# Building the expert-weight table from squared key differences, and conditioning in quarters inside the attention

## The chip, the cores and the metric

The kernel runs on one core of one Trainium2 chip. The metric is device microseconds of one execution, smaller being better. In the profile PE is the matrix engine, DVE the vector engine, ACT the scalar engine, POOL the gather engine and SP the engine that issues the plain DMA transfers. All five run their own instruction streams in program order and wait for one another by semaphores. PSUM is the accumulator memory that PE writes, eight banks of 128x512 float32.

## The reference

Two layers over 512 latent tokens and 256 context tokens of width 1024, float32. Each layer is a conditioned norm, attention (8 heads, 2 key heads), an output projection, a second conditioned norm and a channel mixer that picks experts by product keys:

```python
mod = jax.nn.silu(c) @ ada_w[i] + ada_b[i]          # 6 x 1024 shifts, scales, gates
h = modulate(rms_norm(x, norm1_gain[i]), sh1, sc1)
...
cand_s = (v1[..., :, None] + v2[..., None, :]).reshape(n, PEER_HEADS, PEER_TOPK * PEER_TOPK)
top_s, pos = lax.top_k(cand_s, PEER_TOPK)           # 16 of 128 x 128 experts for each of 8 heads
expert = jnp.take_along_axis(cand_i, pos, axis=-1)
g = jax.nn.softmax(top_s, axis=-1)
act = jax.nn.gelu(jnp.einsum('nhkd,nd->nhk', u_tab[expert], hb))
return jnp.einsum('nhk,nhkd->nd', g * act, v_tab[expert])
```

So every token has 128 (head, rank) slots, each with two keys of 0 to 127 (an expert is 128 times the first plus the second) and a weight g.

## The kernel before

**Layers.** A layer runs qkv, attention, the output projection, the second norm and the expert queries (`peer_q`, with the first top-k), and then mixes experts in two ways at once. The *sparse* way gathers expert rows with POOL (256 context tokens in layer 0, 128 of the 512 latent tokens in layer 1). The *dense* way multiplies all latent tokens that are left (512 in layer 0, 384 in layer 1) with all 16,384 experts: per group of 128 experts, `weights` makes the scores (`sp`, 24 matmuls into PSUM tag "S"), gelu on ACT (`act`), a product with the expert weights `Gt` on DVE, and `outputs` multiplies with the value table (`kp`, `op`). `sp` may run ahead of the rest by LEAD = 5 groups, and by as many `act` buffers as AHEAD gives (2 in layer 0, 12 in layer 1), and `Gt` must have been loaded before the first product.

**The table.** `Gt` is read back from `Gd` in DRAM, which holds for every token a 128x128 table: the sum over the 128 slots of g at (first key, second key). It is built in tiles of 128 tokens, four in layer 0 and three in layer 1, between `peer_q` and the dense work. Per tile `topk_scan` and `topk_resolve` find the slots' keys. `topk_resolve` does so in two passes, i = 0 for the first key and i = 1 for the second: ACT copies the key differences into a large tile `rep` (one buffer), DVE makes a mask `hot` and multiplies the two (2048 elements per partition each), and 16 matmuls add up the result into `keys`. `build_g` then works in rounds of TB = 8 tokens. DVE compares an iota with the keys of 8 tokens (`hot`, bf16, both key sets at once), DVE multiplies the first half with g (`first`, float32), ACT widens the second half (`second`, float32). PE multiplies the two for each token (`gm`, four tokens to a bank of PSUM tag "bg"), and three banks of four are evacuated to `gsb` by ACT, the fourth by DVE. After 32 tokens SP sends `gsb` to `Gd`.

**Conditioning.** `ada_cols` makes 2048 of the 6144 columns of `mod`: 16 loads of 512 KB, 64 matmuls `pr`, a copy `rows`, four transposes `pc` and an add. Layer 0 has groups 0 (at the start), 1 (between qkv and attention) and 2 (in the output projection); the three groups of layer 1 stand behind the first three tiles of layer 0's table.

**Order.** A scheduler in the framework orders each engine's stream when the program is built, from the program's order, its dependences and the buffers. The order is fixed from then on: an engine whose next instruction waits does nothing else.

## Time and profile before

| | us |
|---|---|
| three runs | 4041.8, 4048.7, 4053.2 (median 4048.7) |
| the profiled execution | 4048.4 |
| its span, first to last instruction | 4046.6 |
| PE busy in the span | 3753.2 (93%) |
| DVE busy | 3091.0 (76%) |
| ACT busy | 1536.2 (38%) |
| POOL busy | 1000.8 (25%) |

The span runs through these stages: conditioning and the first norm (0 to 41 us), qkv of layer 0 (41 to 172), conditioning group 1 (to 194), attention (to 336), output projection and norm (to 430), expert queries (to 605), the table (first table matmul at 629.9, last at 880.4), the dense work of layer 0 (to 2290), and in layer 1 the same up to the table (2807.7 to 2993.6) and the dense work (3016.2 to the end). A busy share over the whole span says little, since the stages have different limits, so the rows below are taken by stage. A matmul row may carry several instructions (x16): its duration is then that of the whole burst. Matmuls overlap in the pipeline, so the time that one more costs is the spacing of starts, or a window's PE time over its count, and not the mean duration of one.

### The profile page before, as it was taken

What the parts mean: (1) busy time and instruction counts of PE and PEld (TensorE: products, weight loads), DVE (VectorE), ACT (ScalarE), POOL (GpSimd) and SP (SyncE); (2) the same over time, 40 slices, a digit from 0 to 9 for tenths busy, and PEclk for the clock granted to TensorE, in tenths of its full rate; (3) what the DMA queues carried; (4) which work ended last, traced back from release to release, by engine and by line L of the source; (5) the groups of instructions that cost most, each with busy time, mean ns of one, the idle gap of its engine ahead of it and who ended that gap; (6) DMA issues with size and microseconds to landing.
All of it is one profiled execution on the core that took longest, in us unless ns stands there. A gap on an engine that the chain in (4) does not pass through costs nothing.

```text
span 4046.6 us, 52056 instructions
## 1 busy us (share of the span) xinstructions
PE 3753.2 (93%) x19384; PEld 3200.5 (79%) x19384; DVE 3091.0 (76%) x5913; ACT 1536.2 (38%) x2217; POOL 1000.8 (25%) x778
## 2 busy tenths in 40 slices
...
GB/s 176 125 1 115 58 67 268 188 188 174 297 322 316 310 320 329 324 312 317 316 317 319 250 87 52 45 77 46 154 209 245 303 301 297 296 297 297 305 261 157
DMA packets 343407, 894.08 MB, mean 221 GB/s; under 512 B 25968, under 2 KB 145904, under 8 KB 338800
## 3 DMA queue, kind: packets, MB, share of 16 engines
...
## 4 chain that ended last, share of the span: by engine, by line
PE 49%; issue 19%; DVE 13%; DMA 10%; POOL 8%; ACT 2%; POOLq 0%; SPq 0%; DVEq 0%; ACTq 0%
PE sp L170 5%; DMA gv<-v_n,idx 5%; PE sp L168 5%; PE sp L169 5%; DVE first L554 4%; POOL gv L598 4%; POOL gu L598 4%; PE pj L168 4%; PE pj L169 4%; PE pj L170 4%; DMA gu<-u_n,idx 3%; PE kp L682 2%; PE kp L683 2%; PE kp L681 2%; PE op L683 2%
## 5 line engine op out<-in xcount | busy, mean ns | idle before, releaser
L598 POOL DMA_INDIRECT gu<-u_n,idx x384 | 548.8, 1429 | 2670.0 <-DVE idx L578 964.3
L168 PE MATMUL sp<-hil,Uh 128*128 128x512 f32 (+1 forms) x2048 | 750.8, 367 | 29.8 <-ACT act L659 29.5
L169 PE MATMUL sp<-lol,Uh 128*128 128x512 f32 (+1 forms) x2048 | 751.2, 367 | 0.0
L170 PE MATMUL sp<-hil,Ul 128*128 128x512 f32 (+1 forms) x2048 | 747.0, 365 | 2.6 <-DVE Ul L162 2.6
L626 DVE SCALAR_TENSOR_TENSOR acc<-gv,w,acc 128x1024 f32<-128x1024 f32 x381 | 489.5, 1285 | 138.3 <-DMA gv<-v_n,idx 137.6
L667 ACT CAST wh<-act 128x512 fp32r<-128x512 f32 (+1 forms) x256 | 145.0, 567 | 1039.9 <-DVE act L665 1033.3
L598 POOL DMA_INDIRECT gv<-v_n,idx x384 | 448.9, 1169 | 330.8 <-DVE acc L626 220.2
L616 DVE CUSTOM_DVE_ANT_0 gu<-gu,hn 128x1024 f32<-128x1024 f32 x384 | 468.0, 1219 | 66.7 <-DMA gu<-u_n,idx 66.6
L168 PEld LDWEIGHTS sp<-hil,Uh 128*128 128x128 f32 x2048 | 387.4, 189 | 75.9 <-ACT act L659 30.2
L162 DVE TENSOR_TENSOR Ul<-Ur,Uh 128x1024 fp32r<-128x1024 f32 x256 | 312.4, 1221 | 170.8 <-ACT Uh L160 170.7
L682 PE MATMUL kp<-wh,Vl 128*128 128x512 f32 (+1 forms) x1024 | 381.9, 373 | 47.5 <-DVE Vl L162 47.2
L170 PEld LDWEIGHTS sp<-hil,Ul 128*128 128x128 f32 x2048 | 387.3, 189 | 47.1 <-DVE Ul L162 3.9
L169 PEld LDWEIGHTS sp<-lol,Uh 128*128 128x128 f32 x2048 | 387.6, 189 | 38.5
L160 ACT CAST Uh<-Ur 128x1024 fp32r<-128x1024 f32 x256 | 269.0, 1051 | 391.2 <-PE sp L169 384.5
L681 PE MATMUL kp<-wh,Vh 128*128 128x512 f32 (+1 forms) x1024 | 378.5, 370 | 0.8 <-ACT wh L667 0.7
L683 PE MATMUL kp<-wl,Vh 128*128 128x512 f32 (+1 forms) x1024 | 379.1, 370 | 0.0
L681 PE MATMUL op<-wh,Vh 128*128 128x512 f32 (+1 forms) x1024 | 371.3, 363 | 0.6 <-DVE xl L652 0.6
L683 PE MATMUL op<-wl,Vh 128*128 128x512 f32 (+1 forms) x1024 | 370.8, 362 | 0.0
L682 PE MATMUL op<-wh,Vl 128*128 128x512 f32 (+1 forms) x1024 | 370.7, 362 | 0.0
L160 ACT CAST Vh<-Vr 128x1024 fp32r<-128x1024 f32 x256 | 268.7, 1050 | 221.0 <-PE op L683 201.8
L562 PE MATMUL gm<-first,second 128*128 128x128 f32 x1792 | 239.9, 292 | 98.0 <-DVE first L554 88.1
L562 PEld LDWEIGHTS gm<-first,second 128*128 128x128 f32 x1792 | 223.9, 204 | 126.8 <-ACT second L557 79.3
...
## 6 DMA issues: line engine op xcount, KB each, us to landing
Ur<-u_t SPq DMA_DIRECT2D x256, 512.0 KB, 6.0
Vr<-v_b SPq DMA_DIRECT2D x256, 512.0 KB, 6.8
...
```

The costliest lines, as they stand in the source:

```text
L160: A.copy(hi, raw)
L162: V.tensor_tensor(lo, raw, hi, ALU.subtract)
L168: T.matmul(o, sh, mh, start=i == 0, stop=False)
L169: T.matmul(o, sh, ml, start=False, stop=False)
L170: T.matmul(o, sl, mh, start=False, stop=i == n - 1)
L562: T.matmul(po[:, i * P:(i + 1) * P], second[:, k], first[:, k], start=True, stop=True)
L598: G.indirect_dma_start(out=r, out_offset=None, in_=tab, in_offset=bass.IndirectOffsetOnAxis(ap=idx[:, s:s + 1], axis=0))
L616: V.tensor_tensor_reduce(out=r, in0=r, in1=hn, scale=1.0, scalar=0.0, op0=ALU.mult, op1=ALU.add, accum_out=sd[:, k:k + 1])
L626: V.scalar_tensor_tensor(acc[ti], r, w[:, k:k + 1], acc[ti], ALU.mult, ALU.add)
L681: T.matmul(o[:, :n], vh[:, k, ds], wh, start=start, stop=False, skip_group_check=True)
L682: T.matmul(o[:, :n], vl[:, k, ds], wh, start=False, stop=False, skip_group_check=True)
L683: T.matmul(o[:, :n], vh[:, k, ds], wl, start=False, stop=stop, skip_group_check=True)
```

## The change

Three things change.

**The table.** The one-hot rows no longer come from a comparison with an iota. The `keys` matmuls swap their operands, so that keys come out with tokens instead of slots on the partitions. Five bf16 rows per token are made from the keys k: k, the high and low part of k squared, and two rows of ones (`kd`). They go to DRAM (`kdd`) and come back for each block of 32 tokens with five rows of each of four tokens on 20 partitions (`lk`, one load for each of the two key sets). A constant matrix `sqr` holds 2a, -1, -1 and the parts of -a squared, so that one bf16 matmul `df` of 512 columns gives -(k-a) squared for four tokens. DVE reads the first bank and makes `first` = (df == 0) times g in one instruction; ACT reads the second and makes `second` = relu(df + 1). Rounds have four tokens instead of eight, `first` and `second` three buffers instead of two. The `df` banks have the PSUM tags "O" and "S", and "S" is also that of `sp`.

**Conditioning.** Group 1 of layer 0 and the three groups of layer 1 are cut into quarters (16 matmuls, four loads of 512 KB), and one quarter is placed behind every second query tile of the latent attention in layer 0, sixteen in all.

**Smaller edits.** AHEAD is 3 instead of 2 in layer 0. The pool of the weights is closed before the table is built, and `sparse_prep` loses a copy and two transposes.

```diff
-AHEAD = (2, 12)
+AHEAD = (3, 12)
...
+    def ada_quarters(todo, pool):
+        parts = [(l, grp, q) for l, grp in todo for q in range(4)]
+        loads = []
+        def load():
+            l, grp, q = parts[len(loads)]
+            raws = []
+            for j in range(4):
+                tag, n = ("wr", WR) if len(loads) % 2 == 0 else (("wh", 2), ("wl", 2))[j // 2]
+                raw = pool.tile([P, 2, CBA], F32, tag=tag, name=nm(tag), bufs=n)
+                dma(raw, ada_w[l, grp * 4 + j, :, 2 * q:2 * q + 2])
+                raws.append(raw)
+            loads.append(raws)
+        state = [0, None]
+        def step():
+            i = state[0]
+            state[0] += 1
+            if i >= len(parts):
+                return
+            if i == 0:
+                load()
+                load()
+            l, grp, q = parts[i]
+            pr = bank("S", nm("pr"), 2)
+            for kt in range(2):
+                for j in range(4):
+                    js = slice(32 * j, 32 * j + 32)
+                    T.matmul(pr[js], cst[:, 2 * q + kt], loads[i][j][:, kt], start=kt == 0, stop=kt == 1,
+                             skip_group_check=True)
+            if len(loads) < len(parts):
+                load()
+            if q == 0:
+                state[1] = pool.tile([P, CBA], F32, tag="rows", name=nm("rows"), bufs=1)
+                A.copy(state[1], pr)
+                return
+            rows = state[1]
+            V.tensor_tensor(rows, rows, pr, ALU.add)
+            if q == 3:
+                ada_spread(l, mods[l], grp, rows)
+        return step
...
 def attention(...): ... for qt in range(nt):
+                if beside and qt % 2 == 1:
+                    beside()
...
 def topk_resolve(...): ...
-                T.matmul(ps_[:, i * P:(i + 1) * P], flat(rep[:, a]), identb, start=a == 0, stop=a == 15,
+                T.matmul(ps_[:, i * P:(i + 1) * P], identb, flat(rep[:, a]), start=a == 0, stop=a == 15,
...
-    def build_g(pt, Gd, t, gp, kp):
-        ib = gp.tile([P, 2, P], BF16, tag="ib", name=nm("ib"), bufs=2)
-        A.copy(ib.rearrange("p a b -> p (a b)"), pt[:, :2 * P])
+    def build_g(pt, Gd, t, gp):
+        kd = gp.tile([P, KINDS, 2, P], BF16, tag="kd", name=nm("kd"), bufs=1)
+        both = pt[:, :2 * P].rearrange("p (m s) -> p m s", m=2)
+        A.copy(kd[:, 0], both)
+        kf = gp.tile([P, 2, P], F32, tag="kf", name=nm("kf"), bufs=1)
+        A.copy(kf, both)
+        V.tensor_tensor(kf, kf, kf, ALU.mult)
+        A.copy(kd[:, 1], kf)
+        V.tensor_tensor(kd[:, 2], kf, kd[:, 1], ALU.subtract)
+        V.memset(kd[:, 3:], 1.0)
+        kdd = dram.tile([P, KINDS, 2, P], BF16, tag="kdd", name=nm("kdd"), bufs=2)
+        dma(kdd, kd)
-        HT = TB // 2
+        NB = GB // TQ
...
         for b in range(P // GB):
             gs = gp.tile([P, NK, GB], F32, tag="gsb", name=nm("gsb"), bufs=GSB)
-            for n8 in range(GB // TB):
-                tok = slice(b * GB + n8 * TB, b * GB + (n8 + 1) * TB)
-                hot = kp.tile([P, 2, NK, TB], BF16, tag=("hot", "rep")[n8 % 2], name=nm("hot"), bufs=1)
-                V.tensor_tensor(hot, iota_t[:, None].to_broadcast([P, 2, NK, TB]),
-                                ib[:, :, None, tok].to_broadcast([P, 2, NK, TB]), ALU.is_equal)
-                first = gp.tile([P, TB, NK], F32, tag="first", name=nm("first"), bufs=2)
-                V.tensor_tensor(first, hot[:, 0].rearrange("p a t -> p t a"),
-                                gt[:, tok, None].to_broadcast([P, TB, NK]), ALU.mult)
-                second = gp.tile([P, TB, NK], F32, tag="second", name=nm("second"), bufs=2)
-                A.copy(second, hot[:, 1].rearrange("p a t -> p t a"))
-                for half in range(2):
-                    po = bank("bg", nm("gm"), 4)
-                    for i in range(HT):
-                        k = half * HT + i
-                        T.matmul(po[:, i * P:(i + 1) * P], second[:, k], first[:, k], start=True, stop=True)
-                    pending.append((po, gs, (n8 * 2 + half) * HT, b))
-                    if len(pending) > LAG:
-                        evacuate()
+            lk = gp.tile([KR + 32, NB, P], BF16, tag="lk", name=nm("lk"), bufs=2)
+            for m in range(2):
+                dma(lk[32 * m:32 * m + KR],
+                    kdd[b * GB:(b + 1) * GB, :, m].rearrange("(n t) k s -> (t k) n s", t=TQ))
+            for n4 in range(NB):
+                tok = slice(b * GB + n4 * TQ, b * GB + (n4 + 1) * TQ)
+                dif = []
+                for m, tag in enumerate(("O", "S")):
+                    d_ = bank(tag, nm("df"), 2)
+                    rows = slice(32 * m, 32 * m + KR)
+                    T.matmul(d_, lk[rows, n4], sqr[rows], start=True, stop=True)
+                    dif.append(d_)
+                first = gp.tile([P, TQ, NK], F32, tag="first", name=nm("first"), bufs=3)
+                V.scalar_tensor_tensor(first, dif[0].rearrange("p (t a) -> p t a", t=TQ), 0.0,
+                                       gt[:, tok, None].to_broadcast([P, TQ, NK]), ALU.is_equal, ALU.mult)
+                second = gp.tile([P, TQ, NK], F32, tag="second", name=nm("second"), bufs=3)
+                A.activation(second, dif[1].rearrange("p (t a) -> p t a", t=TQ), AF.Relu, bias=onec)
+                po = bank("bg", nm("gm"), 4)
+                for i in range(TQ):
+                    T.matmul(po[:, i * P:(i + 1) * P], second[:, i], first[:, i], start=True, stop=True)
+                pending.append((po, gs, n4 * TQ, b))
+                if len(pending) > LAG:
+                    evacuate()
...
-            if L == 0:
-                ada_cols(0, modT, 1, wp, ada_load(0, 1, wp, 0))
+                beside = ada_quarters([(0, 1), (1, 0), (1, 1), (1, 2)], wp)
-                attention(LAT, L, blocks_global, *r, ap, False)
+                attention(LAT, L, blocks_global, *r, ap, False, beside)
...
+        wp_es.close()
-        if last:
-            wp_es.close()
-                build_g(pt, Gd, t - c0 // P, gp, kt)
-                if not last:
-                    if t < 3:
-                        ada_cols(1, mods[1], t, wp, ada_load(1, t, wp, 0))
-        if not last:
-            kt_es.close()
-            wp_es.close()
+                build_g(pt, Gd, t - c0 // P, gp)
...
+    a = np.arange(NK)
+    aa = (a * a).astype(np.float32)
+    hi = ((aa.view(np.uint32) + 0x8000) & 0xFFFF0000).astype(np.uint32).view(np.float32)
+    kinds = np.stack([2 * a, -np.ones(NK), -np.ones(NK), -hi, hi - aa]).astype(np.float32)
+    sqk = np.zeros((TQ, KINDS, TQ, NK), np.float32)
+    for i in range(TQ):
+        sqk[i, :, i] = kinds
+    arrays["sqk"] = sqk.reshape(KR, TQ * NK)
```

**Inside a tile of the table, PE.** `gm` are the table's matmuls (x4 is four tokens) and `sp` the score matmuls of the dense work of layer 1. Before, in layer 1's second tile:

```order
L562 MATMUL gm_22085<-first_22076,second_22078 128x128 x4
L562 MATMUL gm_22097<-first_22093,second_22095 128x128 x4
L562 MATMUL gm_22103<-first_22093,second_22095 128x128 x4
L170 MATMUL sp_23132<-hil_17935,Ul_23130 128x384
L168 MATMUL sp_23132<-hil_17935,Uh_23128 128x384
L169 MATMUL sp_23132<-lol_17936,Uh_23128 128x384
L170 MATMUL sp_23132<-hil_17935,Ul_23130 128x384
L168 MATMUL sp_23132<-hil_17935,Uh_23128 128x384
L169 MATMUL sp_23132<-lol_17936,Uh_23128 128x384
L562 MATMUL gm_22115<-first_22111,second_22113 128x128 x4
L562 MATMUL gm_22121<-first_22111,second_22113 128x128 x4
```

and now, in a tile of layer 0 (LDWEIGHTS brings `lk` for the `df` matmul behind it):

```order
L623 LDWEIGHTS lk_6432
L623 MATMUL df_6492<-sqr,lk_6432 128x512
L632 MATMUL gm_6472<-first_6468,second_6470 128x128 x4
L632 MATMUL gm_6486<-first_6482,second_6484 128x128 x4
L623 LDWEIGHTS lk_6432
L623 MATMUL df_6494<-sqr,lk_6432 128x512
L623 LDWEIGHTS lk_6432
L623 MATMUL df_6506<-sqr,lk_6432 128x512
L623 LDWEIGHTS lk_6432
L623 MATMUL df_6508<-sqr,lk_6432 128x512
L623 LDWEIGHTS lk_6432
L623 MATMUL df_6520<-sqr,lk_6432 128x512
```

No `sp` stands among the `gm` or ahead of them any more, in either layer: in both, all 120 matmuls of the first five groups stand behind the last `gm`. Four `df` for the next eight tokens stand ahead of each pair of `gm`, except the `df` in tag "S" of the pair that comes next, which is first behind the pair before it.

**Inside a tile, ACT.** `gsb` is an evacuation of four tokens. Before, in layer 1:

```order
L557 CAST second_21752<-hot_21748 128x1024
L557 CAST second_21771<-hot_21767 128x1024
L541 COPY gsb_21747<-gm_21754 128x128x4
L541 COPY gsb_21747<-gm_21761 128x128x4
L541 COPY gsb_21747<-gm_21773 128x128x4
L557 CAST second_21789<-hot_21785 128x1024
L557 CAST second_21807<-hot_21803 128x1024
L541 COPY gsb_21747<-gm_21791 128x128x4
L541 COPY gsb_21747<-gm_21797 128x128x4
L541 COPY gsb_21747<-gm_21809 128x128x4
```

and now, in layer 0:

```order
L629 ACTIVATE second_6470<-df_6466,onec 128x512
L629 ACTIVATE second_6484<-df_6480,onec 128x512
L606 COPY gsb_6431<-gm_6472 128x128x4
L629 ACTIVATE second_6498<-df_6494,onec 128x512
L629 ACTIVATE second_6512<-df_6508,onec 128x512
L606 COPY gsb_6431<-gm_6500 128x128x4
L606 COPY gsb_6431<-gm_6514 128x128x4
L629 ACTIVATE second_6526<-df_6522,onec 128x512
L629 ACTIVATE second_6540<-df_6536,onec 128x512
L606 COPY gsb_6431<-gm_6528 128x128x4
```

The evacuation of a `gm` stands ahead of the `second` for the next pair, one evacuation in one pair and two in the next.

**Between two tiles, ACT and DVE.** `hot` in these rows is the large tile of `topk_resolve`. Before, in layer 1, from the evacuation to the next tile's `second`, ACT has:

```order
L489 ACT_TABLE_LOAD
L489 ACTIVATE ts_20075<-ts_20075 128x128
L160 CAST Uh_22904<-Ur_22902 128x1024
L659 ACT_TABLE_LOAD
L659 ACTIVATE act_22787<-sp_22762 128x384
L509 CAST rb_21625<-low_21619 128x128
L513 COPY hot_21649<-k_4185_21615 128x2048
L499 CAST k_4288_22013<-i_3896_20078 128x128
L530 CAST ib_21671<-keys_21627 128x256
L532 COPY gt_21673<-keys_21627 128x128
L557 CAST second_21680<-hot_21676 128x1024
L557 CAST second_21697<-hot_21693 128x1024
```

and now, in layer 0, from the last evacuation of a tile:

```order
L606 COPY gsb_6431<-gm_6528 128x128x4
L568 COPY hot_6626<-k_1394_6592 128x2048
L554 CAST k_1583_7170<-i_737_3587 128x128
L568 COPY hot_7183<-dif_7167 128x2048
L587 CAST kd_6648<-keys_6604 128x256
L589 COPY kf_6650<-keys_6604 128x256
L597 COPY gt_6658<-keys_6604 128x128
L591 CAST kd_6648<-kf_6650 128x256
L629 ACTIVATE second_6670<-df_6666,onec 128x512
```

DVE has there before, ahead of the first `first` of the next tile:

```order
L516 TENSOR_TENSOR hot_21649<-hot_21649,hot_21651 128x2048
L453 MAX_INDEX pos_20080<-ts_20079,scr_21989 128x8
L450 MAX_INDEX pos_20080<-ts_20079,cand_21971 128x8
L451 MATCH_REPLACE scr_21995<-ts_20079,cand_21971 128x72
L487 COPY gs_22001<-ts_20079 128x8
L162 TENSOR_TENSOR Ul_22833<-Ur_22829,Uh_22831 128x1024
L452 MAX ts_20079<-scr_21995 128x8
L551 TENSOR_TENSOR hot_21676<-iota_t,ib_21671 128x2048
L551 TENSOR_TENSOR hot_21693<-iota_t,ib_21671 128x2048
L554 TENSOR_TENSOR first_21678<-hot_21676,gt_21673 128x1024
```

and now:

```order
L606 COPY gsb_6431<-gm_6542 128x128x4
L571 TENSOR_TENSOR hot_6626<-hot_6626,hot_6628 128x2048
L570 TENSOR_TENSOR hot_7185<-posb_7172,first_pos 128x2048
L571 TENSOR_TENSOR hot_7183<-hot_7183,hot_7185 128x2048
L590 TENSOR_TENSOR kf_6650<-kf_6650 128x256
L570 TENSOR_TENSOR hot_7206<-rb_7180,rank 128x2048
L592 TENSOR_TENSOR kd_6648<-kf_6650,kd_6648 128x256
L593 MEMSET kd_7226 128x512
L626 SCALAR_TENSOR_TENSOR first_6668<-df_6664,gt_6658 128x512
```

The tile behind the next one (hot_7183, hot_7185, hot_7206) has its masks made here, ahead of the `kf` and `kd` instructions of the next tile (number 6648 and 6650), on both engines. On SP `kdd` is followed by two loads `lk` for each 32 tokens.

## Rows read from the trace of the kernel before

**Rows 1.** Busy time by stage (instructions in brackets), granted clock, DMA share, GB/s

```profile
core 0: us, PE busy (x) PEld busy (x) DVE busy (x) ACT busy (x) POOL busy (x), PEclk, DMA share, GB/s
193.70:336.00 142.30, 131.50 (x580) 83.64 (x579) 102.01 (x338) 85.39 (x227) 0.00 (x0) 0.99 0.04 13
629.90:880.40 250.50, 195.30 (x1355) 160.59 (x1355) 245.68 (x290) 201.87 (x196) 0.00 (x0) 0.92 0.65 196
880.40:908.00 27.60, 7.86 (x25) 6.25 (x26) 17.23 (x96) 10.37 (x15) 0.00 (x0) 0.63 0.89 304
908.00:2290.00 1382.00, 1330.59 (x5766) 1079.82 (x5765) 1121.84 (x1475) 375.10 (x504) 628.33 (x504) 0.99 0.86 304
2807.70:2993.60 185.90, 132.81 (x982) 123.73 (x983) 183.46 (x202) 153.68 (x151) 0.00 (x0) 0.96 0.50 142
2993.60:3016.20 22.60, 14.63 (x77) 13.87 (x75) 15.09 (x62) 11.96 (x17) 0.00 (x0) 0.81 0.95 312
3016.20:4046.60 1030.40, 1018.23 (x5844) 1014.46 (x5843) 789.37 (x1065) 363.19 (x490) 358.71 (x256) 1.00 0.79 276
```

**Rows 2.** Groups of instructions by shape, 605 to 3016 us: busy, mean ns | idle before

```profile
L562 PE MATMUL gm<-first,second 128*128 128x128 f32 x1792 | 239.9, 292 | 98.0 <-DVE first L554 88.1 <-DVE gsb L541 4.8 <-ACT second L557 3.4
L554 DVE TENSOR_TENSOR first<-hot,gt 128x1024 f32<-128x1024 bf16 x112 | 225.4, 2018 | 0.0
L541 ACT COPY gsb<-gm 128x512 f32<-128x512 f32 x168 | 97.3, 593 | 43.7 <-PE gm L562 41.7
L652 DVE SCALAR_TENSOR_TENSOR xl<-op,mod,xl 128x512 f32<-128x512 f32 x128 | 95.2, 744 | 17.5 <-PE op L683 17.5
L516 DVE TENSOR_TENSOR hot<-hot,hot 128x2048 bf16<-128x2048 bf16 x18 | 22.0, 1220 | 4.7 <-ACT hot L513 4.7
L513 ACT COPY hot<-k 128x2048 bf16<-128x2048 bf16 x10 | 19.0, 1898 | 4.8 <-PE keys L518 4.8
```

**Rows 3.** PE over time: start, duration, instruction [idle before <-releaser], layer 1's tiles

```profile
2856.91 2.02 PE L562 MATMUL gm<-first,second 128*128 128x128 f32 x16 [0.50 <-DVE ts L452]
...
2862.75 1.07 PE L518 MATMUL keys<-identb,hot 128*128 128x128 bf16 x16
...
2869.39 1.89 PE L518 MATMUL keys<-identb,hot 128*128 128x128 bf16 x16 [3.15 <-DVE hot L516]
...
2876.44 3.90 PE L562 MATMUL gm<-first,second 128*128 128x128 f32 x32
...
2925.05 2.02 PE L562 MATMUL gm<-first,second 128*128 128x128 f32 x16 [0.50 <-DVE first L554]
```

**Rows 4.** PE over time, start of layer 0's table

```profile
629.88 6.41 PE L562 MATMUL gm<-first,second 128*128 128x128 f32 x32 [3.51 <-DVE first L554]
```

**Rows 5.** ACT over time, between two tiles of layer 1

```profile
2871.52 0.37 ACT L530 CAST ib<-keys 128x256 bf16<-128x256 f32 x1 [3.65 <-PE keys L520]
```

**Rows 6.** ACT reading a PSUM bank with a pointer operand, by line, 41 to 336 us

```profile
L312 ACT ACTIVATE qTl<-pj,qkg 128x512 f32<-128x512 f32 x8 | 5.5, 683 | 0.0
```

**Rows 7.** Chain of waits: stores to DRAM of 512 KB and of 2048 KB

```profile
2676.07 2.84 DMA h_d<-hnat
...
881.17 10.14 DMA Gd<-gsb
```

**Rows 8.** PE over time: conditioning groups 1 and 2 of layer 0

```profile
182.20 1.80 PE L200 MATMUL pr<-wr,cst 128*32 128x512 f32 x6
...
193.17 0.66 PE L206 MATMUL pc<-ident,rows 128*128 128x128 f32 x4 [0.68 <-ACT rows L203]
...
385.33 7.07 PE L200 MATMUL pr<-ar,cst 128*32 128x512 f32 x64
```

**Rows 9.** The `sp` instructions alone by stage: PE, PEld, ACT busy, clock

```profile
629.90:880.40 250.50, 26.72 (x96) 18.34 (x96) 1.19 (x2) 0.92 0.65 196
2700.00:2807.70 107.70, 23.46 (x122) 21.41 (x122) 1.95 (x4) 0.98 0.15 47
2807.70:2993.60 185.90, 30.42 (x148) 26.64 (x149) 3.54 (x7) 0.96 0.50 142
```

44 lines of the change are left out of this document (22 added, 22 removed).

## The prediction

> **What bounds the kernel now.** I read the stage table first. In the dense work PE is nearly always busy: 1330.59 of 1382 us in layer 0 and 1018.23 of 1030.4 in layer 1 [rows 1]. One matmul less there is one matmul sooner, at 1330.59/5766 = 0.231 us for 512 columns and 1018.23/5844 = 0.174 us for 384. The latent attention too is mostly PE, 131.50 of 142.3, with 10.8 us idle. The table is another matter. In its two windows (250.5 and 185.9 us) DVE is busy for 245.68 and 183.46, PE for 195.30 and 132.81, ACT for 201.87 and 153.68 [rows 1]. In the groups, `gm` waits 98.0 us in all, 88.1 of it for `first` on DVE, and DVE has 2018 ns of `first` for eight tokens and the `hot` besides [rows 2]. So DVE sets the table's pace, and this is what the change attacks.
>
> PE's time in those windows is not all the table's. 96 `sp` (26.72 us) lie inside layer 0's table, and 122 + 148 ahead of and inside layer 1's [rows 9]: dense work done free of charge while DVE is late. They stop being free if they are pushed out.
>
> A tile's body, from the first `gm` at 2876.44 to the end of the last burst at 2925.05 + 2.02, takes 50.6 us [rows 3]. That leaves between tiles (250.5 - 4 x 50.6)/3 = 16.0 us in layer 0 and (185.9 - 3 x 50.6)/2 = 17.0 in layer 1. The gap shown, 2858.93 to 2876.44, is 17.5 [rows 3].
>
> **Part 1, a pair of `gm` (eight tokens).** A further 16 passes of `gm` cost (3.90 - 2.02) = 1.88 us [rows 3]. The four new `df` of 512 columns are priced from the `sp` spacing at 0.231 each (from the 16 `keys` of 128 columns, 1.07/16 x 4 = 0.27), so PE alone needs 1.88 + 0.92 = 2.80 a pair. DVE needs two reads of a bank, at 744 ns for an op of that form, and a share of the evacuations: it drops to half. ACT needs two `second`, at 683 ns (a read of a bank with a pointer operand) [rows 6], and one or two evacuations at 593 [rows 2]: under 2.6. By throughput PE would be the bound. But the streams have a fixed order. An evacuation stands on ACT ahead of the next pair's `second`, and `gm` of that pair needs that `second`. Where ACT evacuates the second bank of a pair, a pair takes the whole loop: `gm` 1.88, evacuation 0.59, `second` 0.68 and two handovers of some 0.1, 3.35 in all. Where DVE takes that bank, the `df` in tag "S" stands behind the `gm`: 1.88 + 0.23 + 0.68 + 0.3 = 3.1. The mean is 3.22, and a tile's body 15 x 3.22 + 1.88 = 50.2, against 50.6: **no gain**, though DVE is freed.
>
> The Trainium skill ("ScalarE: Activation LUTs", Rules for kernel authors) says to do a relu on VectorE, which it has as up to three times as fast per element in bf16. For a float32 bank of PSUM the rows say otherwise: 744 ns on DVE, 683 on ACT [rows 2, 6]. Still, by that rule `second` would leave ACT's queue, a pair would take the four DVE reads, 2.98, and the seven tiles some 25 us less, 4103 in all.
>
> **Part 2, between tiles.** The chain after the last `gm` is now: `keys` 1.07, ACT's copy 1.90, DVE's product 1.22, `keys` 1.89 [rows 2, 3], with handovers 6.6. Then ACT's copy and DVE's product for the tile behind the next, 1.90 + 1.22, which stand in front; then three small steps of at most 0.37 each [rows 5] and one more mask, 1.22, that stands between them: with handovers 6.0. Then two trips through DRAM, `kdd` and `lk`, each taken as the 512 KB store, 2.84 [rows 7]: 5.7. Then `df` and `second`, 1.2. That is 19.5, and 15.2 for the last gap of a layer, where no tile is behind the next (4.3 less). The trips are the uncertain piece, since no load in 256-byte pieces is in the trace. With `lk` at nothing the gap is 16.7; with `kdd` as slow as the 2048 KB store `Gd`, 10.14 [rows 7], it is 27. I stay with 2.84, since `kdd` has 328 KB.
>
> The Trainium skill ("DMA: Bandwidth & Descriptors", Specifications and Anatomy of one DMA) gives a fixed 2.0 us per DMA and wants 512 bytes for line rate, and the `lk` pieces have 256. Its fit would make an estimate of 2.75 + 2.09 = 4.8 us for both trips and the sum 6 us less; the row with 2.84 is in line with it, and no row shows the penalty for small pieces.
>
> Two more things belong here. In the gap PE did `sp` before, and the burst after it ran at full pace (32 in 3.90, 2876.44). Now PE has only `keys` there, and the nearest row for a start out of idleness is 629.88: 32 in 6.41 [rows 3, 4], 2.5 us more. And the first `gm` of a layer waits for kd, both trips and `df` (12.9) instead of `ib`, `hot` and `second` (5.2 from the end of the second `keys` to the `gm` at 2876.44): 7.7 later in layer 0, and in layer 1, where DVE is behind with top-k, between 2 and 7.7, taken as 5.
>
> Layer 0: 7.7 + (2 x 19.5 + 15.2 - 48.1) + 3 x 2.5 - 4 x 0.4 = **+20** (from -25 to +50). Layer 1: 5 + (34.7 - 34.1) + 2 x 2.5 - 3 x 0.4 = **+9** (from -25 to +30).
>
> **Part 3, the dense work behind the table.** The order has no `sp` ahead of the last `gm` any more, since `df` holds tag "S", and 120 behind it. In layer 0 this costs nothing. The handover there takes 27.6 us, of which PE is busy for 7.86 [rows 1], the rest being the trip of `Gd` to `Gt`, and the third `act` buffer lets 120 `sp` (27.7) run in it. **0** (to +5). In layer 1 AHEAD was 12 all along. Before, 270 + 77 = 347 `sp` are done when `kp` begins (77 in the handover, clock 0.81) [rows 1, 9]; now 120. The missing 227 come back inside a stage that is PE from end to end: 227 x 0.174 = 39.5. The handover is 22.6 long, and 120 x 0.174 = 20.9 fit. **+40** (25 to 47).
>
> **Part 4, conditioning.** A group is 64 matmuls, 7.07, and four transposes, 0.66 [rows 8]. Three groups lay inside layer 0's table, where PE had time. Now four lie in the attention, 30.9 us of PE. Group 1 no longer stands alone: 182.20 to 193.7 [rows 1, 8], and about 2 us of its matmuls before that, 13.5. Of the 10.8 us that PE idles in the attention I let them fill 6. **+11** (+5 with all 10.8 filled, +17 with none). Their transfers take 64 loads of 512 KB, 33.6 MB, which at 304 GB/s [rows 1] is 110 us, less than the stage, in which the queues now carry 13 GB/s.
>
> The copy and two transposes taken out of `sparse_prep` lie beside the dense work: 0 to -1.
>
> **The sum** starts from the profiled execution, 4048.4 us (span 4046.6 and 1.8 around it; the median of the runs is 4048.7): 4048.4 + 11 + 20 + 0 + 9 + 40 = **4128**.
>
> **Rivals.**
> *The build falls to PE's own work.* This is the reading by busy shares: DVE is the bound, PE next. The windows of the table then hold 195.30 - 26.72 (`sp`) - 23.2 (three conditioning groups) + 256 x 0.231 (`df`) = 204.5 of 250.5, and 132.81 - 30.42 (`sp` again) + 192 x 0.231 = 146.7 of 185.9 [rows 1, 8, 9]: 85 us gained. With +11 and +40 this gives 4048.4 - 85 + 51 = 4014, **faster**. It decides from about 7 us saved per tile with its gap (50 of the 85 over seven tiles). For it: 88.1 of 98.0 us of waits name `first`. Against it: the order on ACT, and a chain between tiles that PE cannot shorten. Chance 0.15.
>
> *Only the pair reaches PE's floor*, because handovers and `second` overlap better than I add them: 15 x 2.80 + 1.88 = 43.9 a tile, 6.3 less in seven tiles, 44 us: 4084. Chance 0.14.
>
> *The quarters come late.* They are sixteen waits on PE's queue with the rest of attention behind them. If each stalls by as much as one quarter's transfer (2.1 MB at 304 GB/s, 6.9 us) exceeds the two-quarter lead, some 2 us, it adds 34: 4162. For it: SP issues in order, and each load waits for a buffer that an earlier step frees. Against it: two quarters are loaded ahead and a head takes about 16 us. Chance 0.11.
>
> **How the numbers follow.** Forecast 0.60. Differences under 0.3% (12 us) cannot be told from no change. The forecast's own range, 4095 to 4160, is all slower. The first rival is faster but for a small part, the second slower or same. Faster 0.14, same 0.09, slower 0.77. The range leaves out most of the first rival and a little above the third: 4040 to 4175.
>
> **What would show it.** In the new trace: `gm` in pairs about 3.2 us apart, idle before them put down to ACT's `second` and not to DVE; DVE near half busy in the table; gaps of 17 to 24 us between tiles with only `keys` on PE; no `sp` in the table's windows; 120 `sp` in layer 1's handover and a dense stage there of about 1070 us; attention near 160 us with 16 steps of `pr`. I am wrong if pairs come 2.8 apart, if gaps are near 10, or if layer 1's dense stage does not grow.

## The result and the profile after

The changed kernel takes 4197.6 us (median of four runs, 4188.6 to 4208.7), the kernel before 4047.5 beside it: a ratio of 1.0372, 95% interval 1.0342 to 1.0402. It is slower by 150 us. The forecast was 4128, slower, with a range that ended at 4175, so the sign was right and the size about half of what came. The profiled execution took 4194.0 us, with a span of 4192.1.

The timelines of the two profiles, read at the same events, show where the time went (us from the start of each span):

| event | before | after | later by | of this, in the stage |
|---|---|---|---|---|
| conditioning in the output projection, layer 0 | 385.3 | 424.1 | 38.8 | 38.8 |
| last matmul of the expert queries, layer 0 | 603.1 | 644.8 | 41.7 | 2.9 |
| first `gm`, layer 0 | 629.9 | 679.9 | 50.0 | 8.3 |
| last `gm` ends | 880.4 | 939.5 | 59.1 | 9.1 |
| first `kp` | 908.0 | 967.4 | 59.4 | 0.3 |
| last `kp` of layer 0 | 2368.5 | 2438.2 | 69.7 | 10.3 |
| last matmul of the expert queries, layer 1 | 2772.4 | 2846.1 | 73.7 | 4.0 |
| first `gm`, layer 1 | 2807.7 | 2891.1 | 83.4 | 9.7 |
| last `gm` ends | 2993.5 | 3080.6 | 87.1 | 3.7 |
| first `kp` | 3016.2 | 3101.8 | 85.6 | -1.5 |
| last `kp` | 4040.4 | 4186.1 | 145.7 | 60.1 |

The largest shares are the dense work of layer 1 (60.1, forecast 40) and the front up to the end of the expert queries (41.7, forecast 11); the dense work of layer 0 (10.3) had no term in the forecast. The two tables, from the expert queries to the last `gm`, carry 17.4 and 13.4 and are near what was forecast. (The dense work of layer 0 ends with its last `kp`, in before at 2368.9 and not at 2290.)

The stage table of after has the same columns as [rows 1]; its first row is the latent attention.

```profile
core 0: us, PE busy (x) PEld busy (x) DVE busy (x) ACT busy (x) POOL busy (x), PEclk, DMA share, GB/s
200.90:375.00 174.10, 151.34 (x782) 80.44 (x781) 97.95 (x295) 74.38 (x188) 0.00 (x0) 1.00 0.52 189
679.90:939.50 259.60, 183.88 (x1376) 139.84 (x1376) 124.16 (x236) 147.71 (x248) 0.00 (x0) 0.91 0.44 132
939.50:967.40 27.90, 27.90 (x122) 22.43 (x121) 21.23 (x92) 16.47 (x22) 0.00 (x0) 1.00 0.83 289
2891.10:3080.60 189.50, 137.69 (x1023) 105.39 (x1023) 82.86 (x128) 108.18 (x179) 0.00 (x0) 0.91 0.43 130
3080.60:3101.80 21.20, 21.20 (x121) 20.91 (x119) 13.85 (x56) 13.89 (x19) 0.00 (x0) 1.00 0.88 312
```

DVE, busy for 245.68 of 250.5 us in layer 0's table before [rows 1], is now busy for 124.16 of 259.6: the change did what it says, DVE is free, and the table takes longer. Both handovers (rows three and five) are about as long as before (27.6 and 22.6) with PE busy throughout, on 120 `sp`. The latent attention, from 211.4 to 336 before, fills 174 us. The same view of before for that stretch and, behind it, what PE waited for in it after (us in all, times, the longest):

```profile
211.40:336.00 124.60, 115.90 (x504) 72.16 (x503) 85.35 (x273) 70.97 (x184) 0.00 (x0) 0.99 0.02 5
```

```profile
PE sc L421 <- ACT pr L438: 11.4, 7, 1.7
PE pt L453 <- DVE mx L429: 5.1, 4, 1.3
PE pr L251 <- DVE pT L460: 2.1, 4, 0.5
...
```

PE has 35.4 us more work there and idles for 22.8 instead of 8.7: the waits of the scores (`sc`) for the softmax and of the transposes (`pt`) for the maximum have grown, and new ones for the copies out of tag "S" have come. (`pr` of L438 is the softmax's tile, `pr` of L251 the accumulator of the quarters.)

Inside a tile the timeline of PE shows pairs of `gm` 3.3 us apart (start, duration, instruction, idle before), here in the first tile:

```profile
689.90 2.05 PE L632 MATMUL gm<-first,second 128*128 128x128 f32 x16 [0.73 <-ACT second L629]
691.88 0.60 PE L623 MATMUL df<-sqr,lk 20*128 20x512 bf16 x4
693.22 2.05 PE L632 MATMUL gm<-first,second 128*128 128x128 f32 x16 [0.73 <-ACT second L629]
```

In the first tile every pair takes 3.32 us; in the six others pairs of 3.32 and 3.21 us alternate, but for the slow ones at a tile's start. ACT in such a tile shows why:

```profile
776.78 0.59 ACT L606 COPY gsb<-gm 128x512 f32<-128x512 f32 x1 [0.67 <-PE gm L632]
778.05 1.27 ACT L629 ACTIVATE second<-df,onec 128x512 f32<-128x512 f32 x2 [0.69 <-PE df L623]
779.98 0.59 ACT L606 COPY gsb<-gm 128x512 f32<-128x512 f32 x1 [0.67 <-PE gm L632]
780.88 0.59 ACT L606 COPY gsb<-gm 128x512 f32<-128x512 f32 x1 [0.31 <-PE gm L632]
781.36 1.27 ACT L629 ACTIVATE second<-df,onec 128x512 f32<-128x512 f32 x2
```

Where DVE takes the pair's second bank, ACT idles for 0.69 us until PE has made the `df`, and the pair takes 3.21; where ACT takes it, `second` stands behind that evacuation, and the pair takes 3.32.

Between two tiles there is a gap of 16.8 us, first on PE, then on DVE:

```profile
734.01 1.06 PE L573 MATMUL keys<-hot,identb 128*128 128x128 bf16 x16
738.31 1.86 PE L573 MATMUL keys<-hot,identb 128*128 128x128 bf16 x16 [3.25 <-DVE hot L571]
...
749.04 1.96 PE L623 MATMUL df<-sqr,lk 20*128 20x512 bf16 x5 [8.65 <-DMA lk<-kdd]
750.97 3.78 PE L632 MATMUL gm<-first,second 128*128 128x128 f32 x16
```

```profile
744.75 0.42 DVE L592 TENSOR_TENSOR kd<-kf,kd 128x256 bf16<-128x256 f32 x1
...
747.56 0.48 DVE L593 MEMSET kd<- 128x512 bf16 x1 [2.12 <-DMA kdd<-kd]
```

The last part of `kd` is done at 745.17, `kdd` has been stored by 747.56 and `lk` is there at 749.04: 2.4 and 1.5 us for the two trips, where the forecast took 2.84 each. The burst behind the gap then takes 3.78 us for 16, against 2.05 later. The granted clock is why: in the gap PE is nearly idle (busy for 0.39 us from 740 to 749), the clock in the burst is 0.50 (1.2 GHz), and behind it 1.00 (2.4 GHz):

```profile
751.00:754.60 3.60, 3.60 (x17) 3.45 (x16) 0.69 (x1) 1.08 (x2) 0.00 (x0) 0.50 0.01 2
754.70:765.00 10.30, 8.22 (x65) 6.01 (x64) 4.84 (x8) 6.53 (x11) 0.00 (x0) 1.00 0.04 8
```

### The profile page after: what moved, and what is told of

Same layout as the page of the kernel before. It is cut to its first block, busy times and chain, and to the rows that moved or that the text cites. A ratio compares the mean times of both kernels' runs of the same rounds, so it can differ in the third digit from the quotient of the medians.

```text
span 4192.1 us, 53315 instructions
## 1 busy us (share of the span) xinstructions
PE 3837.3 (92%) x19826; PEld 3213.3 (77%) x19826; DVE 2916.6 (70%) x5949; ACT 1451.9 (35%) x2331; POOL 997.6 (24%) x777
## 3 DMA queue, kind: packets, MB, share of 16 engines
q0 software_dynamic: 110592, 402.70, 27.6%
## 5 line engine op out<-in xcount | busy, mean ns | idle before, releaser
L746 PE MATMUL op<-wh,Vh 128*128 128x512 f32 (+1 forms) x1024 | 376.4, 368 | 10.6 <-DVE xl L717 10.6
L169 DVE TENSOR_TENSOR Vl<-Vr,Vh 128x1024 fp32r<-128x1024 f32 x256 | 311.3, 1216 | 8.5 <-ACT Vh L167 8.2
```

The costliest lines, as they stand in the source:

```text
L169: V.tensor_tensor(lo, raw, hi, ALU.subtract)
L746: T.matmul(o[:, :n], vh[:, k, ds], wh, start=start, stop=False, skip_group_check=True)
```

## The experiments

Twelve kernels were run, each beside the kernel before on the same chip. Ratios are to that kernel, with their 95% intervals:

| run | median us | ratio (interval) |
|---|---|---|
| the changed kernel | 4197.6 | 1.0372 (1.0342 to 1.0402) |
| quarters_only | 4077.2 | 1.0073 (1.0056 to 1.0090) |
| table_only | 4219.4 | 1.0423 (1.0405 to 1.0440) |
| after_shift | 4194.0 | 1.0366 (1.0348 to 1.0383) |
| after_df_bg | 4166.3 | 1.0296 (1.0279 to 1.0314) |
| after_second_dve | 4204.9 | 1.0397 (1.0377 to 1.0417) |
| after_made_ahead | 4143.4 | 1.0241 (1.0218 to 1.0263) |
| after_pr_o | 4183.9 | 1.0344 (1.0322 to 1.0367) |
| combo | 4069.2 | 1.0050 (1.0024 to 1.0076) |
| after_df_ahead | 4153.4 | 1.0264 (1.0248 to 1.0280) |
| after_sparse_early | 4163.2 | 1.0289 (1.0271 to 1.0307) |
| combo_df_s0 | 4003.3 | 0.9900 (0.9885 to 0.9915) |
| before_sparse_early | 4034.0 | 0.9963 (0.9950 to 0.9975) |

**The two parts by themselves: quarters_only and table_only.** The edit of the first:

```diff
-            if L == 0:
-                ada_cols(0, modT, 1, wp, ada_load(0, 1, wp, 0))
...
+                beside = ada_quarters([(0, 1), (1, 0), (1, 1), (1, 2)], wp)
-                attention(LAT, L, blocks_global, *r, ap, False)
+                attention(LAT, L, blocks_global, *r, ap, False, beside)
...
-                        ada_cols(1, mods[1], t, wp, ada_load(1, t, wp, 0))
```

> The kernel before with the conditioning alone moved into the attention (sixteen quarters; the table as before). Theory from the trace of after: a head of the latent attention takes 21.2 us instead of 14.1 there, and the output projection's conditioning starts 38.8 us later. If the quarters alone do this, this kernel shows the same 21 us a head, about 39 us more up to the output projection, and 30 to 40 us in all, since the groups taken out of layer 0's table lay where PE had time: about 4083. Rival, the forecast's term: +11 us, about 4058. Second rival: the loss comes from something else in the changed kernel's front, and this one stays at 4047.

It measured 4077.2, some 30 us more. Its heads come 20.2 and 22.5 us apart in turn, as in after, where before they came 14.1 apart, and its first `gm` is 35.4 us later than before. Its table for layer 0 then takes 251.8 us, against 250.5: taking three conditioning groups out of it gave nothing back, which fits the rows of before, in which they lay in time that PE waited for DVE.

The second has the new `build_g`, `topk_resolve` and `sparse_prep`, and all else as before, AHEAD of 2 and the pools among it:

> The kernel before with the new table alone (conditioning where it was, AHEAD 2 and 12, pools as before; the constant sqr is staged through the tile of the sub-keys to fit the memory). Theory: what is left of after's 4195 without the 39 us of the quarters, 4156, with pairs of gm 3.3 us apart, no sp ahead of layer 1's last gm, and layer 1's dense stage some 1080 us long. Rival: the two parts hinder one another, and without the quarters it is nearer to the forecast's 4117 (4128 less 11).

It measured 4219.4, which neither side had expected: without the quarters the new table is slower still, by 22 us. The gaps of layer 0 are 36.8 to 41.4 us long (in layer 1, where no conditioning stands between tiles, 13.3 and 16.1). PE in one of them, cut:

```profile
708.19 5.50 PE L207 MATMUL pr<-wr,cst 128*32 128x512 f32 x15 [7.75 <-DMA wr<-ada_w]
...
720.24 1.06 PE L525 MATMUL keys<-hot,identb 128*128 128x128 bf16 x16
724.54 1.05 PE L525 MATMUL keys<-hot,identb 128*128 128x128 bf16 x16 [3.25 <-DVE hot L523]
```

The whole conditioning group stands on PE between the last `gm` and the next tile's `keys`, with the wait for the second half of its loads. So the quarters cost about 30 us by themselves and, with AHEAD 3 and the pools, save about 22 next to the new table; the two effects do not add.

**Where the operand lies: after_shift.**

```diff
-    onec = const.tile([P, 1], F32, name="onec")
-    V.memset(onec, 1.0)
...
-                A.activation(second, dif[1].rearrange("p (t a) -> p t a", t=TQ), AF.Relu, bias=onec)
+                A.activation(second, dif[1].rearrange("p (t a) -> p t a", t=TQ), AF.Relu, bias=ones[:, :1])
```

> The changed kernel with one constant of one column left out (relu's bias is a column of the tile of ones), so that every tile behind it lies 32 bytes lower in the memory, and the operand hi and lo of the scores again at an address that is 32 more than a multiple of 64, as before. Nothing else differs. In after's trace the sp starts are 2 to 3 per cent further apart than in before's (0.2300 against 0.2239 us in layer 0, 0.1744 against 0.1709 in layer 1, by the same count), while kp and op are not. Theory: this comes from where the operand lies; then sp goes back to before's spacing and the time falls by 3072 times 0.006 and 0.0035, some 25 us, to 4170. Rival: the spacing has another cause and stays, 4195.

The spacing went back. In 300 us of layer 1's dense work (the stage view, from 3500 to 3800), before, after and after_shift in this order:

```profile
3500.00:3800.00 300.00, 300.00 (x1727) 300.00 (x1726) 240.46 (x313) 108.19 (x148) 124.57 (x86) 1.00 0.85 298
...
3500.00:3800.00 300.00, 300.00 (x1716) 300.00 (x1715) 239.04 (x308) 107.16 (x145) 125.18 (x86) 1.00 0.85 298
...
3500.00:3800.00 300.00, 300.00 (x1727) 300.00 (x1726) 240.18 (x312) 108.27 (x146) 124.86 (x86) 1.00 0.85 300
```

The time did not go down as expected. In layer 1 the dense stage took 1072.6 us instead of 1084.3. In layer 0 PE was busy for 13.6 us less, but waited that much longer, above all for `Vl` (36.6 against 26.0). The median, 4194.0, cannot be told from 4197.6. So about 11 us of the loss lie in layer 1's `sp` by the trace, and the times do not decide it.

**The head start: after_df_bg.**

```diff
-                for m, tag in enumerate(("O", "S")):
-                    d_ = bank(tag, nm("df"), 2)
+                for m, tag in enumerate(("bg", "bg")):
+                    d_ = bank(tag, nm("df"), 4)
...
-                po = bank("bg", nm("gm"), 4)
+                po = bank("O", nm("gm"), 2)
```

> The changed kernel with the accumulator banks swapped: the squared differences take the four banks of gm, gm the two of tag O, and tag S is left to sp. In the order sp stands in the table again, one to four between the pairs, and in the gaps. Theory: layer 1's loss (58 us from first kp to the end against before) is the lost head start, so it falls away but for the part that before did ahead of the table; 45 to 60 us less, 4140 to 4150, with pairs of gm still 3.3 us apart, since sp lies in PE's waits. Rival: the pairs become longer by what sp takes (2 on average, 0.35 us), half of the gain is lost, 4165.

It measured 4166.3, 31 us under after. With tag "S" left to them, 351 `sp` stand ahead of layer 1's first `kp` (344 before, 120 in after), and from there to the last `kp` it takes 1048.1 us instead of 1084.3. Pairs stay at 3.32 us (median), so `sp` does lie in PE's waits. But the first `gm` of layer 1 comes later against the expert queries (52.3 us, 45.0 in after) and the table is 3 us longer. The lost head start is worth 36 us, near the forecast's 40. It does not explain all: with the same head start as before the stage is still 24 us longer. PE idles for 23.9 us of it instead of 8.4, and `sp` keeps after's wider spacing.

**What sets the pair: after_second_dve and after_df_ahead.**

```diff
-                A.activation(second, dif[1].rearrange("p (t a) -> p t a", t=TQ), AF.Relu, bias=onec)
+                V.tensor_scalar(second, dif[1].rearrange("p (t a) -> p t a", t=TQ), 1.0, 0.0, ALU.add, ALU.max)
```

> The changed kernel with relu's work done by DVE (add 1, then maximum with 0, from the same bank); ACT keeps the evacuations only. In after a pair of gm takes 3.31 us, PE waits 0.62 to 0.73 of it for second on ACT, and DVE is busy for less than half. Theory: the pair is a loop through ACT, evacuation and then second; with second on DVE nothing of ACT's stands ahead of it, the pair is set by four reads of a bank on DVE at 0.64 and one evacuation of four at 0.69, some 2.8 to 2.9, near PE's own 2.55 to 2.8, and 105 pairs give 45 us: 4150. Rival: the loop only changes engines (gm, then its wait for a bank or for DVE's queue), pairs stay at 3.3 and the time at 4195.

It measured 4204.9, no faster. Pairs of 3.21 and 3.50 us now alternate:

```profile
775.73 2.02 PE L632 MATMUL gm<-first,second 128*128 128x128 f32 x16 [0.65 <-DVE second L629]
776.10 1.49 DVE L626 SCALAR_TENSOR_TENSOR first<-df,gt 128x512 f32<-128x512 f32 x2
777.68 0.61 PE L623 MATMUL df<-sqr,lk 20*128 20x512 bf16 x4
777.79 0.69 DVE L606 COPY gsb<-gm 128x512 f32<-128x512 f32 x1 [0.20 <-PE gm L632]
778.40 1.28 DVE L629 TENSOR_SCALAR second<-df 128x512 f32<-128x512 f32 x2
779.22 2.02 PE L632 MATMUL gm<-first,second 128*128 128x128 f32 x16 [0.94 <-DVE second L629]
781.18 0.61 PE L623 MATMUL df<-sqr,lk 20*128 20x512 bf16 x4
781.60 1.29 DVE L629 TENSOR_SCALAR second<-df 128x512 f32<-128x512 f32 x2 [0.52 <-PE df L623]
```

The evacuation ahead of `second` has not gone: where DVE takes a bank it now stands ahead of `second` on DVE, whose work in such a pair (0.69, 1.28 and 1.49) fills 3.46 of the 3.50 us. In the other pairs nothing stands ahead of `second`, and DVE idles for 0.52 us until PE has made the `df`: 3.21 us, as in after where ACT idles for it. So there are two loops of nearly the same length, and taking away the longer one, on ACT, could give at most 0.11 us in some of the pairs. The run does not show that the evacuation is harmless, only that a second limit lies right behind it: PE's order, in which the `df` of the next `second` stands behind the `gm` of this pair. The next edit makes the products two rounds behind their `df`:

```diff
+        def products():
+            first, second, gs, o, b = ready.pop(0)
...
-                po = bank("bg", nm("gm"), 4)
-                for i in range(TQ):
-                    T.matmul(po[:, i * P:(i + 1) * P], second[:, i], first[:, i], start=True, stop=True)
-                pending.append((po, gs, n4 * TQ, b))
-                if len(pending) > LAG:
-                    evacuate()
+                ready.append((first, second, gs, n4 * TQ, b))
+                if len(ready) > 2:
+                    products()
+        while ready:
+            products()
```

> The changed kernel with the products gm of four tokens written two rounds behind their df, first and second, nothing else; in the order PE now has two df, then the gm of four tokens, in turn, instead of four df behind each pair of gm. With second moved to DVE the pairs stayed at 3.2 to 3.5 us, so the theory that ACT's evacuation ahead of second sets the pace has fallen. New theory: the loop is PE's own order. The df of the next second stands behind the gm of this pair, so PE must wait for df, bank read and handover (0.6 to 0.7) once a pair, whichever engine reads. With df two rounds ahead that wait goes, a pair takes PE's 1.99 + 0.60 = 2.6, and 105 pairs save 70 us: 4125. Rival: three buffers of first and second and two banks per tag are too few, the wait only moves: 3.1 to 3.3 a pair, 4180 to 4195.

It measured 4153.4, 44 us under after. PE no longer waits inside a tile:

```profile
700.18 1.16 PE L608 MATMUL gm<-first,second 128*128 128x128 f32 x8
701.27 0.39 PE L634 MATMUL df<-sqr,lk 20*128 20x512 bf16 x2
701.59 1.16 PE L608 MATMUL gm<-first,second 128*128 128x128 f32 x8
...
703.00 1.16 PE L608 MATMUL gm<-first,second 128*128 128x128 f32 x8
```

Four tokens take 1.41 us, a pair 2.82, PE's own work with no idle time before either burst. The tables take 238 and 170 us instead of 260 and 190. The edit ends both loops at once: the `df` run two rounds ahead of their `gm`, and with them `second` stands ahead of the evacuation that it waited for. So it does not tell the two apart. The expected 2.6 was too low since PE now goes from `gm` to `df` and back twice a pair: a step from `gm` to `gm` is 0.11 us, one from the last `gm` to `df` 0.21.

**Between tiles: after_made_ahead.** `topk_scan`, `topk_resolve` and the making of `kd` and `kdd` of the next tile are written behind half of a tile:

```diff
+            if b == 2:
+                halfway()
...
+            make(c0 // P)
             for t in range(c0 // P, NLAT // P):
-                topk_scan(tk["l", t], v12["l", t], 1, kt)
-                pt = topk_resolve(tk["l", t], i12["l", t], kt, "bg", lambda i, shape: kt.tile(
-                    shape, BF16, tag=("hot", "rep")[i], name=nm("hot"), bufs=1))
-                build_g(pt, Gd, t - c0 // P, gp)
+                build_g(made[t], Gd, t - c0 // P, gp, lambda: make(t + 1))
```

> The changed kernel with the next tile's top-k, keys, kd and its trip through DRAM written behind the first two quarters of a tile instead of behind the whole tile; in the order the keys of the next tile now stand between the gm of this one. After has gaps between tiles of 13.4 to 16.8 us, 76.8 in all five, of which PE waits 8.7 for lk alone in a gap. Theory: DVE and ACT have room for this work beside the pairs, the gaps fall to 2 or 3 us each and some pairs get longer by the copies of 1.9 us on ACT (twice a tile): 76.8 - 12 - 20, some 45 us less, 4150. Rival: the work is on ACT, which sets the pairs' pace, and all of it comes back as longer pairs: 4185 to 4195.

It measured 4143.4, 54 us under after, a little more than expected. No gap of over 6 us is left in either table, and they take 226.8 and 168.0 us instead of 259.6 and 189.5. The gaps shrink by 71 us in all (76.8 to 6.0), and the work that left them comes back in part: most pairs stay at 3.2 to 3.3 us, some take 5 to 6, and the bodies of the tiles grow by 10.7 us in layer 0 and 5.6 in layer 1.

**The bank of the quarters: after_pr_o.**

```diff
-            pr = bank("S", nm("pr"), 2)
+            pr = bank("O", nm("pr"), 2)
```

> The changed kernel with the accumulator of the quarters (pr) in tag O, whose banks only the head's outputs use, instead of tag S, which the transposes pt of every query tile use. In after the latent attention takes 174 us instead of 125, 35 of the difference PE's own work and 14 more waiting: 11.4 for the softmax on ACT, 5.1 for the maximum on DVE, 4.6 for copies out of tag S. Theory: the quarters hold banks of tag S and push the transposes and with them the next scores back; with tag O the added waiting goes, 10 to 14 us less, 4183. Rival: the waiting comes from where the quarters stand in PE's order, whatever bank they use: no change, 4195.

The stage table of the latent attention (after: 174.10 us, PE busy for 151.34):

```profile
201.30:363.50 162.20, 154.87 (x776) 81.33 (x775) 100.86 (x294) 73.28 (x188) 0.00 (x0) 1.00 0.57 204
```

PE idles there for 7.3 us instead of 22.8, about as long as before (8.7). So the added waiting came from sharing the banks of tag "S". Heads come 17.8 and 21.4 us apart in turn instead of 20.2 and 22.5, and the last matmul of the expert queries comes 10.1 us earlier, as expected. The median, 4183.9, is 13.7 us lower, but the intervals overlap and the profiled execution gives the 10 us back later, so what the times show of it stays open.

**The late gathers: after_sparse_early and before_sparse_early.** The top-k of the tiles that are mixed by the sparse way is placed by an offset counted in scheduling steps:

```diff
-SLACK2 = 800
+SLACK2 = 0
```

> The changed kernel with the sparse tiles' top-k and keys put at their place in the program instead of 800 scheduling steps behind it (SLACK2 0); in the order their keys then stand ahead of the first kp of either layer, not behind some ten groups of it. In after POOL's gathers start 103 us behind the first kp in layer 1 (25 in before), while DVE's instructions that wait for them keep their places among those that PE needs; PE waits there for xl in layer 0 (10.6 us) and for Ul and Vl in layer 1 (18.5 idle in the first 300 us, against 8.4). Theory: the late gathers cause these waits; with early keys the idle time of the dense stages falls by some 20 us, against 5 to 10 us more until the first kp, since DVE does the top-k in the handover: 4180 to 4185. Rival: the top-k in the handover holds Gt's product on DVE for its 20 us and costs as much as it gives or more: 4195 to 4215.

It measured 4163.2, 34 us under after and better than expected. Of the 28.6 us between the two profiled executions 21.5 lie in the dense work of layer 1. The cause is in the stage view around the first `kp` of layer 1, in which POOL's busy time starts with the gathers; first before (`kp` from 3016.2), then after (`kp` from 3101.8):

```profile
3016.20:3040.00 23.80, 23.64 (x152) 22.82 (x152) 23.70 (x68) 12.04 (x19) 0.00 (x0) 0.97 0.67 235
3040.00:3060.00 20.00, 18.40 (x102) 17.24 (x101) 12.66 (x21) 6.29 (x9) 7.43 (x7) 1.00 0.79 287
...
3180.00:3200.00 20.00, 20.00 (x117) 20.00 (x116) 10.73 (x13) 6.82 (x8) 0.00 (x0) 1.00 0.39 127
3200.00:3220.00 20.00, 20.00 (x128) 18.13 (x127) 10.70 (x16) 6.07 (x9) 6.38 (x6) 1.00 0.64 221
```

The first gather starts 108 us behind `kp` instead of 28. The instructions on DVE that use the gathers keep their places among those that PE needs, so DVE waits for a gather (`gu`, 21.9 us up to 3400, 1.1 in after_sparse_early) and PE for DVE. What PE waited for in layer 1 from the first `kp` to 3400, in after and then in after_sparse_early:

```profile
PE sp L177 <- DVE Ul L169: 9.2, 1, 9.2
PE kp L747 <- DVE Vl L169: 4.8, 3, 3.6
PE kp L746 <- ACT wh L732: 3.4, 1, 3.4
...
PE kp L746 <- ACT Vh L167: 3.9, 1, 3.9
PE keys L573 <- DVE hot L571: 1.0, 1, 1.0
```

18.8 us (with a wait of 1.4 not shown) became 4.9, of which 3.9 stand ahead of the first `kp`. In layer 0 one wait goes and another comes; first after, then after_sparse_early:

```profile
PE op L746 <- DVE xl L717: 10.6, 5, 4.0
...
PE keys L573 <- DVE hot L571: 14.3, 3, 10.6
```

Its dense stage there is 4.9 us shorter than in after, and still 5.4 longer than before.

> The kernel before with SLACK2 0 and nothing else, to tell what of the version that took 4003 (45 us under the kernel before) is the new table's and what is the place of the sparse keys, which alone took 34 us off the changed kernel. Theory: in the kernel before the gathers start 25 us behind the first kp of layer 1 already, and PE waits 8 us there and 40 in layer 0 for Vl, so there is little to gain: 4035 to 4050, and most of the 45 us belong to the table. Rival: the early keys free the dense stages here as they did there, 4015 or less, and the new table, with all its repairs, is worth some 10 us.

The same edit takes the kernel before to 4034.0, about 15 us less, of which 11 lie in its dense work of layer 0.

**A version that is faster: combo and combo_df_s0.** Both have the new table with after_df_bg's banks and after_made_ahead's order, group 1 of the conditioning where it was before, and the three groups of layer 1 as twelve quarters between the pairs of layer 0's table. AHEAD is 2 in layer 0, and the constant of one column is left out. The second has after_df_ahead's and after_sparse_early's edits besides. The place of the quarters:

```diff
+                if beside and n4 % 8 == 5:
+                    beside()
```

> A version put together from what the runs so far point to: the new table with its squared differences in the four banks of gm and gm in tag O (sp stands in the table again), the next tile's keys made half a tile ahead, conditioning of layer 0 where it was before, and the three groups of layer 1 as twelve quarters between the pairs of layer 0's table, one or a few matmuls at a time, where PE waits 0.6 to 0.7 us a pair; no constant of one column. Theory, from the kernel before (4046): the front and the dense stages as before; pairs as before in length; five gaps of 16 to 17 us shrink to some 3 and grow pairs by 20 in all; the first gm of each layer 8 later and slow starts 5: 4046 - 68 + 20 + 16 + 5 = 4020, faster by 0.6%. Rival: quarters and keys lengthen the pairs by all that they take (21 + 45), no gain: 4050 to 4080.

It measured 4069.2. Its tables take 237 and 167 us, but its first `gm` come 12 and 9 us later against the expert queries than before, partly since quarters and `sp` stand ahead of them, and its dense stages are 10 and 22 us longer, with waits like those of after (10.9 us of `op` for `xl` in layer 0).

> The version put together before, with the products two rounds behind their df and with the sparse keys at their place. The version without these two took 4069: its tables took 237 and 167 us (250 and 186 in the kernel before), but its first gm came 15 and 10 us later and its dense stages were 10 and 22 us longer, the waits of the late gathers. Theory: pairs at 2.6 to 2.7 take another 25 to 30 us out of the tables, of which layer 1 gives back some 15 to 20, since less sp fits between the pairs; early gathers give back 20 of the dense stages: 4069 - 55 + 18 - 20 = 4010, faster by 0.9%. Rival: the head start is lost in full (39 us) and the top-k in the handover costs 20: 4075.

It measured 4003.3, faster than the kernel before by 1.0% (0.85 to 1.15). The stage view of its two tables:

```profile
644.20:852.60 208.40, 206.30 (x1490) 146.74 (x1490) 129.70 (x225) 149.02 (x249) 0.00 (x0) 0.99 0.76 225
2784.40:2930.30 145.90, 145.56 (x1041) 109.64 (x1040) 91.06 (x149) 108.94 (x182) 0.00 (x0) 0.99 0.63 177
```

PE is busy for 206.30 of 208.4 and 145.56 of 145.9 us. Of the 45 us to the kernel before about 15 are what the sparse keys' place gives there too. If the two add, which no run shows, about 30 are left to the new table with its order and the conditioning between its pairs.

## Why the prediction was right in sign and wrong in size

**What bounds the kernel.** DVE at 98% did set the table's pace, and freeing it did bring the pace down to the next limit. The forecast's main point held: the next limit was no better. A tile's body was forecast at 50.2 us against 50.6, and the bodies of after run to 52.5 to 54.5, with the slow start that the forecast kept as a term of its own.

**The pair: right, in both its loops.** Forecast were 3.35 us where ACT evacuates the second bank of a pair and 3.1 where DVE does, with a mean of 3.22. Measured are 3.32 and 3.21, in turn in six tiles, and 3.32 throughout in the first. What was expected of after_df_ahead takes the evacuation on ACT for refuted, since after_second_dve was no faster; the traces do not bear that out. Both loops are there, 0.11 us apart, so an edit that ends only one of them gains next to nothing, and after_df_ahead ends both. What the forecast had wrong here is the price of the four `df`, 0.92 us: they take 0.60, since two of 20 rows each run at the same time. PE's own work in a pair is then 1.98 + 0.60 = 2.58, not 2.80. That after_df_ahead came to 2.82 is chance: there the steps between the two kinds of matmul come twice. The rule of the Trainium skill ("ScalarE: Activation LUTs", Rules for kernel authors) that a relu belongs on VectorE would have given 4103 by the forecast's sum; with just that edit the time was 4204.9, and `second` takes 684 ns on DVE and 688 on ACT.

**Between tiles: right.** Gaps of 19.5 and 15.2 were forecast; they are 16.8, 16.0 and 14.4, then 16.1 and 13.4, a little under the 17 to 24 that were named as the sign. The term that was most too large was the trips, 5.7, which took 3.9. The fit of the Trainium skill ("DMA: Bandwidth & Descriptors", Anatomy of one DMA), which it gives for DMAs on the path of the gather engine while these are issued by SP, makes an estimate of 4.8 for the two: nearer, and too long as well. The slow start is there, 3.78 us for the first 16 at a granted clock of 0.50 against 2.05 at 1.00, 1.7 a tile instead of 2.5. First `gm`: 8.3 and 9.7 later, forecast 7.7 and 5. Together layer 0's table was forecast at +20 and came at 17.4, layer 1's at +9 and came at 13.4.

**Handovers: right.** 0.3 and -1.5 us, 120 `sp` in each. The third `act` buffer, which the forecast gave as the reason in layer 0, was not needed: table_only, with AHEAD 2, runs 120 there too, in 27.9 us.

**The head start: right, within what it priced.** Forecast +40, and the count bears it out: 6053 PE instructions between the first and the last `kp` of layer 1 against 5831, 222 x 0.174 = 38.6 (the head start before was 344 `sp`; the forecast's 347 counts three twice, at the edges of its windows). after_df_bg gave 36 of it back. The stage grew by 60.1. The failed step is what the forecast left out: that nothing else changes "inside a stage that is PE from end to end". The idle time in it grew by 10.5 (18.9 against 8.4), which after_sparse_early removed, and the `sp` got 2% further apart, about 10 us more, which after_shift removed in the trace.

**Layer 0's dense work: missed, and open in part.** No term, +10.3. The loss comes early: 192 `kp` into the stage the changed kernel is 17.6 us behind the kernel before, and it gains some of that back later. In that stretch `op` waits 10.6 us for `xl`, which it did not before, and the keys of the second tile of context tokens come 145 us behind the first `kp` instead of 55, behind 142 `kp` instead of 24. The change does not touch SLACK2, but an offset that counts scheduling steps lands elsewhere when the steps ahead of it change; the order would have shown it. after_sparse_early puts these keys early and has no wait for `xl`, but 14.3 us for the keys, and gets 4.9 of the 10.3 back. The rest stays open. It is not the wider spacing of `sp`: in after_shift PE is busy for 13.6 us less here, and the stage is as long (1471.9 us against 1470.8).

**Conditioning: mis-sized, +11 against +41.7 up to the end of the expert queries.** Its work was priced at 30.9 and PE's busy time in the attention rose by 35.4. The step that failed is "of the 10.8 us that PE idles in the attention I let them fill 6". They filled nothing; idle time rose by 14.1, which makes 20 of the 31 us that were missing. PE's work is 4.5 more than its price, and taking out the group that stood alone let the latent attention start 10.5 us earlier, not 13.5. The 14.1 come from the shared banks of tag "S": in after_pr_o, with tag "O", PE idles for 7.3 us, and the front is 10 us shorter. But there too the quarters fill hardly any of the 8.7 us that were idle before: a matmul in PE's order does not go to where PE waits. quarters_only measured the part by itself, 30 us in the time and 35 up to the first `gm`. The third rival (late loads) had the place right and the reason wrong: PE waits for no load there.

**The range** ended at 4175. The three misses, 31, 10 and 20 us, have one sign, and the range had none of them: it took each stage that the change does not touch as unchanged, and let the added PE work in the attention cost at most its own time. That the sign came out right rests on the head start and the tables, whose terms held.

**The first rival** (4014, PE's own work alone) was rightly put low for this kernel. The tables of combo_df_s0, 208.4 and 145.9 us with PE busy throughout, are close to its 204.5 and 146.7. That the whole time comes near, 4003.3, is chance: the sum has `df` too dear, no quarters in the table, the 40 us for the head start and nothing for the sparse keys' place.
